# A bidirectional SSD layer: turnings of a tile in one step, TensorE's order tied at each chunk's scores, context products inside the main products

## The chip, the core and the metric

One core of a Trainium2 chip runs the kernel. The core has five engines with a queue of instructions each: TensorE (PE, matrix products and transposes by a product with the identity), VectorE (DVE), ScalarE (ACT), GpSimd (POOL) and SyncE (SP, which issues DMAs). Each engine takes its instructions in the order of its queue and waits on semaphores for the results of the others. The metric is the device time of one execution in microseconds. 0.5% of it is 9 us.

## The reference

Two layers over 1024 latent positions of width 1024 and a prefix of 256 context positions: layer 0 is gated windowed attention, layer 1 a gated bidirectional Mamba-2 mixer (SSD). Only layer 1 matters here. Per head group g of 8 (four heads of 64, state 128, chunks of 128):

```python
def ssd_mixer(h_lat, h_ctx, w_in, conv_w, conv_b, dt_bias, a_log, d_skip, norm_w, w_out, need_ctx_out):
    def front(h):
        z, xbc, dt_raw = jnp.split(h @ w_in, [SSD_WIDTH, SSD_WIDTH + SSD_CONV_DIM], axis=-1)
        xbc = jax.nn.silu(centred_depthwise_conv(xbc, conv_w, conv_b))   # 5 taps
        xs, bm, cm = jnp.split(xbc, ...)
        ...
    z_c, xs_c, b_c, c_c, dt_c = front(h_ctx)
    z, xs, bm, cm, dt = front(h_lat)
    y_c_f, s_f = scan_dir(xs_c, b_c, c_c, dt_c, 0, h0, need_ctx_out)
    y_c_b, s_b = scan_dir(xs_c, b_c, c_c, dt_c, 1, h0, need_ctx_out)
    y_f, _ = scan_dir(xs, bm, cm, dt, 0, s_f, True)
    y_b, _ = scan_dir(xs, bm, cm, dt, 1, s_b, True)
    # back: u = (y_f + y_b + d_skip * xs) * silu(z), RMS norm per group, @ w_out
```

A chunk's output is y_diag, the product of the scores cm @ bm^T (weighted by decays) with xs, and y_off, the product of cm with the state ahead of the chunk. The context gives the states with which the two scans begin.

## The kernel before

Every product in float32 is made of three products of split halves: weight high by input high, weight high by input low, weight low by input high (`wh`, `wl` and `uH`, `uL`).

For each group g, the generator `front(g)` makes what the scan needs. It has four tiles of 128 channels, in the order bT, x0, x1, cT, and then two gate tiles z. For a tile the *main product* is 48 matmuls of 128x512 over the 1024 latent positions (L1095), into a two-bank PSUM buffer `pj2`, of which there are two. For bT, x0 and x1 there is also a *context product*, 24 matmuls of 128x256 (L1085), into `psD`, one bank of PSUM and the only one of its name. A product is followed by the convolution (first tap on ScalarE, L1007; four taps on VectorE, L1011), by SiLU (tanh on ScalarE, L1018; product on VectorE, L1019) and, for bT, x0 and x1, by `natural`: turnings (transposes by TensorE, L1058) of the channel tile back into position-major form, into the same PSUM buffer, and copies by ScalarE (L1061) into `bn` or `xn`. Each z tile is 96 matmuls of 128x256 (L1129) into `pj2`: the first z tile takes the buffer that tile x1 leaves, the second that of cT. The last two tiles of weights, for z, come as `wr` and are split into `wh` (ScalarE, L1034) and `wl` (VectorE).

The steps behind a product go into a queue `post`, from which `front`'s progress releases them: one step for every 0.5 us of TensorE's products, and `natural`'s steps at least LATE = 3.0 us after the step before them, one a time.

The scan of group g runs in eight calls of `slot`, one for each chunk of 128: the scores (L1247, into a bank of `psX`, of which there are three), the two state reads (L1249, L1250), the state update (L1256, L1257), the multiplication with the decays `M` (L1251; `M` itself comes from `merge` on VectorE, L1230, and from four exponentials on ScalarE, L1236), four products with `xn` (L1281), the gate and the norm (L1292, L1293, L1295, L1300), two transposes of the result (L1312) with a copy each (`uT`, L1313), which is written out by DMA. Between these steps `fill(x)` draws work of `front(g + 1)`, so that TensorE has products to do; in the last group the work is the output projection `ssd_out` (L1527). The states at the chunks' borders (L1198, each into `psD`, then L1202 or L1210) are made by another generator, `states`, once tile x1 has been released.

The program is built by a scheduler: it takes the instructions in program order with their dependencies and buffers, orders each engine's queue by its own estimate of when each could start, and sets the semaphores. So an instruction's place in a queue is not its place in the code. `issue_after` is a tie for the scheduler: what is issued inside it stands behind the named instruction in that instruction's own queue, and no semaphore is added.

## Time and profile before

| | us |
|---|---|
| three runs | 1805.05, 1812.2, 1811.74 (median 1811.74) |
| profiled execution, its time | 1807.02 |
| its span, first to last instruction | 1805.3 |
| attention and the rest ahead of the SSD layer's front(0) | about 0 to 745 |
| front(0), before any scan | about 745 to 849 |
| eight groups' scans, first scores to first scores | 849.3, 954.8, 1060.5, 1166.3, 1272.1, 1377.9, 1483.7, 1589.0 |
| first matmul of the gate tiles, groups 1 to 3 | 924.58, 1030.35, 1136.13 (105.78 apart) |
| last group's scan with the output projection | 1589 to about 1743, then the tail |

Group g's scan and group g + 1's front share a stretch of about 105.8 us. In the profile's rows a line number is that of the kernel before; names like `pj` stand for `pj2`, without buffer numbers; `[1.30 <-ACT xn L1061]` is the time that the engine stood idle ahead of an instruction, and the instruction whose end released it. TensorE's matmuls overlap a little, so the distance between two starts, not the duration, is the time that one costs.

### The profile page before, as it was taken

The page shows a single profiled execution, that of the slowest core. Times are in us where ns is not written, and L with a number is a line of the kernel's source. Part 1 is how long each engine was busy: PE and PEld are TensorE (multiplying, and loading weights), DVE is VectorE, ACT ScalarE, POOL GpSimd, SP SyncE. Part 2 cuts the span into 40 slices and gives each one's busy share as a digit, 9 for nine tenths or more (in the row PEclk, how much of TensorE's full clock was granted, in tenths as well). Part 3 has the DMA queues.
Part 4 walks back from the last instruction along what each step waited for, and adds up shares of the span by engine and source line. Part 5 has one row for each costly group of instructions (what it writes and reads, how often), then busy time and mean ns, then how long its engine had stood idle before and what let it go on. Part 6 is the DMA issues. An engine that isn't in the chain of part 4 may idle for free.

```text
span 1805.3 us, 28983 instructions
## 1 busy us (share of the span) xinstructions
PE 1739.6 (96%) x10319; PEld 1494.7 (83%) x10319; DVE 1181.8 (65%) x2115; ACT 867.1 (48%) x1906; POOL 799.0 (44%) x1068
## 2 busy tenths in 40 slices
PE   6899999999999999999999999999999999999997
PEld 2697788888888887778888898988889898888887
DVE  4634436778877885684776858577684867766734
ACT  3612237777777774452443525344353534544522
POOL 2331127555575545103454544645454464554411
PEclk9999999999999999999999999999999999999999
DMA  9558856444455436222222323222332322656533
GB/s 334 226 144 268 283 177 149 106 100 111 111 153 130 120 102 221 73 53 73 71 77 82 92 62 98 79 71 79 81 93 62 100 73 76 174 169 170 175 101 121
DMA packets 212495, 227.61 MB, mean 126 GB/s; under 512 B 16384, under 2 KB 149632, under 8 KB 212352
## 3 DMA queue, kind: packets, MB, share of 16 engines
q1 hardware_dynamic: 178288, 207.12, 38.0%
q0 software_dynamic: 34064, 18.65, 5.8%
q8 instruction: 81, 1.33, 0.3%
q14 instruction: 62, 0.51, 0.1%
HBM read 190.88 MB, written 35.13 MB: 125 GB/s over the span
## 4 chain that ended last, share of the span: by engine, by line
PE 81%; DVE 9%; ACT 4%; DMA 3%; issue 2%; SPq 1%; POOL 1%; DVEq 0%; ACTq 0%; POOLq 0%
PE pj L1095 17%; PE pj L1129 10%; PE pj L1527 7%; PE pj L246 6%; PE pj L247 6%; PE pj L248 6%; PE psD L1085 4%; PE psX L1281 3%; PE pt L684 3%; PE psD L1198 2%; PE pv L691 2%; PE pv L690 1%; PE S L659 1%; PE S L658 1%; PE psX L1249 1%
## 5 line engine op out<-in xcount | busy, mean ns | idle before, releaser
L246 PE MATMUL pj<-uH,wh 128*128 128x512 f32 (+1 forms) x712 | 257.4, 363 | 9.0 <-ACT uH L470 6.3
L247 PE MATMUL pj<-uL,wh 128*128 128x512 f32 (+1 forms) x712 | 243.3, 342 | 0.5 <-POOL uL L707 0.4
L248 PE MATMUL pj<-uH,wl 128*128 128x512 f32 (+1 forms) x712 | 242.4, 341 | 1.4 <-POOL wl L231 1.4
L1095 PE MATMUL pj<-uH,wl 128*128 128x512 f32 x512 | 172.7, 405 | 0.0
L1095 PE MATMUL pj<-uH,wh 128*128 128x512 f32 x512 | 171.4, 405 | 1.2 <-ACT bn L1061 0.7
L1095 PE MATMUL pj<-uL,wh 128*128 128x512 f32 x512 | 169.2, 402 | 0.0
L246 PEld LDWEIGHTS pj<-uH,wh 128*128 128x128 f32 x712 | 135.6, 191 | 36.2 <-ACT uH L470 7.7
L1129 PE MATMUL pj<-wh,uH 128*128 128x256 f32 x512 | 150.3, 294 | 9.1 <-ACT xn L1061 9.1
L1173 POOL TENSOR_TENSOR xw<-xn,dtdec 128x256 f32<-128x256 f32 x144 | 92.9, 650 | 141.6 <-PE psD L1198 107.1
L1129 PE MATMUL pj<-wh,uL 128*128 128x256 f32 x512 | 152.7, 298 | 0.0
L248 PEld LDWEIGHTS pj<-uH,wl 128*128 128x128 f32 x712 | 135.0, 190 | 18.6 <-POOL wl L231 2.3
L247 PEld LDWEIGHTS pj<-uL,wh 128*128 128x128 f32 x712 | 135.8, 191 | 16.0 <-issue 3.0
L1129 PE MATMUL pj<-wl,uH 128*128 128x256 f32 x512 | 146.7, 287 | 0.0
L689 DVE TENSOR_TENSOR pl<-pt,ph 128x512 fp32r<-128x512 f32 x168 | 114.1, 688 | 47.2 <-ACT ph L688 46.2
L231 POOL TENSOR_TENSOR wl<-wr,wh 128x512 fp32r<-128x512 f32 x76 | 100.2, 1322 | 86.1 <-ACT wh L229 85.2
L663 DVE CUSTOM_DVE_ANT_0 sm<-S,mask,nsink 128x640 f32<-128x640 f32 (+2 forms) x160 | 119.2, 773 | 19.8 <-PE S L659 12.6
L665 ACT ACTIVATE sm<-sm,nm 128x640 f32<-128x640 f32 (+2 forms) x160 | 118.6, 742 | 16.6 <-DVE nm L663 15.9
L688 ACT CAST ph<-pt 128x512 fp32r<-128x512 f32 x168 | 97.5, 586 | 56.0 <-PE pt L684 52.7
L229 ACT CAST wh<-wr 128x512 fp32r<-128x512 f32 (+1 forms) x116 | 74.7, 648 | 87.7 <-PE pj L247 63.5
L1095 PEld LDWEIGHTS pj<-uH,wl 128*128 128x128 f32 x512 | 95.3, 188 | 19.2
L1095 PEld LDWEIGHTS pj<-uL,wh 128*128 128x128 f32 x512 | 95.4, 188 | 18.7
L1129 PEld LDWEIGHTS pj<-wh,uH 128*128 128x128 f32 x512 | 98.7, 193 | 13.5 <-ACT xn L1061 12.1
(339 smaller groups left out, 4810.8 us busy)
## 6 DMA issues: line engine op xcount, KB each, us to landing
wr<-w_x SPq DMA_DIRECT2D x32, 512.0 KB, 4.6
M<-acs SPq DMA_DIRECT2D x64, 256.0 KB, 4.9
bw<-acs SPq DMA_DIRECT2D x64, 256.0 KB, 5.5
wr<-w_sk SPq DMA_DIRECT2D x24, 512.0 KB, 3.8
wr<-wg SPq DMA_DIRECT2D x40, 256.0 KB, 4.5
qs<-q POOLq DMA_DIRECT2D x40, 256.0 KB, 3.9
wada<-w_ada SPq DMA_DIRECT2D x16, 512.0 KB, 7.2
wr<-wq SPq DMA_DIRECT2D x32, 256.0 KB, 3.0
```

Source lines behind the costliest of these rows:

```text
L231: (eng or nc.vector).tensor_tensor(l, raw, h, op=ALU.subtract)
L246: self.nc.tensor.matmul(ps, lh, rh, start=first and i == 0, stop=False)
L247: self.nc.tensor.matmul(ps, lh, rl, start=False, stop=False)
L248: self.last_mm = self.nc.tensor.matmul(ps, ll, rh, start=False, stop=last and i == n - 1)
L663: nc.vector.tensor_tensor_reduce(out=sm[:, :W], in0=Sv, in1=self.mask[:, m0 : m0 + W], scale=-SCALE, scalar=self.nsink[:, 4 * j + r : 4 * ...
L665: nc.scalar.activation(sm[:, :W], sm[:, :W], AF.Exp, bias=nm[:, r : r + 1], scale=-1.0, accum_out=sums[:, r : r + 1])
L688: nc.scalar.copy(ph, ptf)
L689: nc.vector.tensor_sub(pl, ptf, ph)
L1095: nc.tensor.matmul(raw[:, 512 * i : 512 * i + 512], l[:, k, :], r[i][:, k, :], start=k + y == 0, stop=k == KT - 1 and y == 2)
L1129: nc.tensor.matmul(pj[:, c], l, r[:, k, :], start=c % 2 + q + k + y == 0, stop=c % 2 == 1 and q == 1 and k == 3 and y == 2)
L1173: nc.gpsimd.tensor_tensor(xw, X(st, c).rearrange("p (r h) -> p r h", r=R), self.dtdec[:, c, hd(d, g)].unsqueeze(2).broadcast_to([P, R, HP] ...
L1527: nc.tensor.matmul(banks[x], l[:, z, sl], r, start=k == 2 * qs[0] and y == 0, stop=k == 2 * qs[-1] + 1 and y == 2)
```

## The change

Three parts. (1) `natural` makes all turnings of a tile in one step and the copies in the steps behind it, where it made four turnings, a copy, four turnings, a copy. (2) `self.pe` remembers the last product matmul and `self.opened` a chunk's scores: the scores stand behind the last product drawn before them on TensorE's queue, and what a fill draws stands behind the chunk's scores. (3) Except in the very first tile, the context product is drawn in the middle of the tile's main product, ahead of k = 4 of 8, where it was drawn before the main product. The instructions are the same in number and shape.

```diff
--- before.py
+++ after.py
@@ -1051,19 +1051,15 @@
             return lambda: weights(a["w_z"][g, q], 4, 256)
 
         def natural(raw, acc, dst, o, n):
-            steps = []
-
-            def tr(lo, hi):
-                for x in range(lo, hi):
+
+            def tr():
+                for x in range(n):
                     nc.tensor.transpose(raw[:, x * P : (x + 1) * P], acc[:, x * P : (x + 1) * P], self.ident)
 
             def ev(d, lo, hi):
                 nc.scalar.copy(d[:, :, o : o + P], raw[:, lo * P : hi * P].rearrange("p (c n) -> p c n", n=P))
 
-            for d, lo, hi in dst:
-                steps.append(lambda lo=lo, hi=hi: tr(lo, hi))
-                steps.append(lambda d=d, lo=lo, hi=hi: ev(d, lo, hi))
-            return [(LATE, steps)]
+            return [(LATE, [tr] + [lambda d=d, lo=lo, hi=hi: ev(d, lo, hi) for d, lo, hi in dst])]
 
         tiles = [(16 + g, "bT"), (2 * g, 0), (2 * g + 1, 1), (24 + g, "cT")]
         st["xn"] = [t(p, [P, 4, R * HP], F32, "xn4") for _ in range(2)] + [t(p, [P, NCC, R * HP], F32, "xn2")]
@@ -1078,21 +1074,26 @@
             cur, w = w, (weights(a["w_dt"], KT, P) if g + n == 0 else loads[n + 1]())
             nat = {"bT": ("bn", 0), 0: ("xn", 0), 1: ("xn", P)}.get(kind)
             wh, wl = cur["h"], cur["l"]
-            if nat:
-                raw = t(ps, [P, 512], F32, "psD")[:, :CTX]
+            def ctx():
+                cr = t(ps, [P, 512], F32, "psD")[:, :CTX]
                 for k in range(KT):
                     for y, (l, r) in enumerate(((wh, uH), (wh, uL), (wl, uH))):
-                        nc.tensor.matmul(raw, l[:, k, :], r[2][:, k, :], start=k + y == 0, stop=k == KT - 1 and y == 2)
+                        self.pe = nc.tensor.matmul(cr, l[:, k, :], r[2][:, k, :], start=k + y == 0, stop=k == KT - 1 and y == 2)
                         yield N256
                 acc = t(pf, [P, CTX], F32, "cctx")
-                post.extend(self.taps(x, raw, acc, 0, CTX, CTX) + self.silu(raw, acc) + natural(raw, acc, [(st[nat[0]][2], 0, 2)], nat[1], 2))
+                post.extend(self.taps(x, cr, acc, 0, CTX, CTX) + self.silu(cr, acc) + natural(cr, acc, [(st[nat[0]][2], 0, 2)], nat[1], 2))
+
+            if nat and g + n == 0:
+                yield from ctx()
             raw = t(ps, [P, LAT], F32, "pj2")
             acc = t(pf, [P, LAT], F32, "cacc") if nat and kind != "bT" else t(p, [P, LAT], F32, kind)
             for q in ((0,), (1,)) if g == 0 and n == 0 else ((0, 1),):
                 for k in range(KT):
+                    if k == KT // 2 and nat and g + n > 0:
+                        yield from ctx()
                     for y, (l, r) in enumerate(((wh, uH), (wh, uL), (wl, uH))):
                         for i in q:
-                            nc.tensor.matmul(raw[:, 512 * i : 512 * i + 512], l[:, k, :], r[i][:, k, :], start=k + y == 0, stop=k == KT - 1 and y == 2)
+                            self.pe = nc.tensor.matmul(raw[:, 512 * i : 512 * i + 512], l[:, k, :], r[i][:, k, :], start=k + y == 0, stop=k == KT - 1 and y == 2)
                             yield N512
                     if k == 3 and (q[0] == 0 or g + n == 0):
                         post.extend(w["steps"])
@@ -1126,7 +1127,7 @@
                         u, v = uH[i][:, 4 * q + k, c * P : (c + 1) * P], uL[i][:, 4 * q + k, c * P : (c + 1) * P]
                         for y, (l, r) in enumerate(((u, ww["h"]), (u, ww["l"]), (v, ww["h"]))):
 
-                            nc.tensor.matmul(pj[:, c], l, r[:, k, :], start=c % 2 + q + k + y == 0, stop=c % 2 == 1 and q == 1 and k == 3 and y == 2)
+                            self.pe = nc.tensor.matmul(pj[:, c], l, r[:, k, :], start=c % 2 + q + k + y == 0, stop=c % 2 == 1 and q == 1 and k == 3 and y == 2)
                             yield N256
                 if i == 1 and q == 0 and g + 1 < G:
                     st["next"] = weights(a["w_x"][16 + g + 1], KT, P)
@@ -1244,7 +1245,8 @@
             if n + 2 < G * NCH:
                 bw[n + 2] = load_rows(n + 2, 1, "bw")
             pcb = t(ps, [P, 512], F32, "psX")[:, :P]
-            nc.tensor.matmul(pcb, st["bT"][:, cs], st["cT"][:, cs], start=True, stop=True)
+            with self.tc.issue_after(self.pe.ins):
+                self.opened = nc.tensor.matmul(pcb, st["bT"][:, cs], st["cT"][:, cs], start=True, stop=True)
             po = t(ps, [P, 512], F32, "psX")
             nc.tensor.matmul(po[:, :256], st["cT"][:, cs], flat(st["hf"]), start=True, stop=True)
             nc.tensor.matmul(po[:, 256:], st["cT"][:, cs], flat(st["hb"][c]), start=True, stop=True)
@@ -1358,11 +1360,12 @@
                 def run(until):
                     nonlocal spent
                     while spent < until:
-                        cost = next(work, None)
-                        if cost is None:
-                            return
-                        spent += cost
-                        post.run(cost)
+                        with self.tc.issue_after(self.opened.ins):
+                            cost = next(work, None)
+                            if cost is None:
+                                return
+                            spent += cost
+                            post.run(cost)
 
                 def tick():
                     nonlocal chain
@@ -1524,7 +1527,7 @@
                     for x in range(4):
                         sl = slice(x * P, (x + 1) * P)
                         for y, (l, r) in enumerate(((w["h"], hi), (w["h"], lo), (w["l"], hi))):
-                            nc.tensor.matmul(banks[x], l[:, z, sl], r, start=k == 2 * qs[0] and y == 0, stop=k == 2 * qs[-1] + 1 and y == 2)
+                            self.pe = nc.tensor.matmul(banks[x], l[:, z, sl], r, start=k == 2 * qs[0] and y == 0, stop=k == 2 * qs[-1] + 1 and y == 2)
                             yield N512
                         if x == 1 and z == 0 and j < len(ws):
                             post.extend(ws[j]["steps"])
```

What the scheduler makes of it is seen in three places of the built programs. Lines move by a little: L1061 becomes L1060, L1095 L1096, L1085 L1081, L1129 L1130, L1058 L1057, L1198 L1199, L1312 L1314, L1247 L1249, L1236 L1237, L1313 L1315, L1295 L1297, L1202 L1203.

The first place is ScalarE's queue ahead of the gate product of the second of the seven groups after the first. Before, from the copies of tile x1's first four turnings to the copy of its last four:

```order
L1061 COPY xn_2452_10689<-pj_2526_11107 128x4x128
L1061 COPY xn_2454_10691<-psD_11038 128x2x128
L1236 ACTIVATE M_11231<-M_11231,vf_8731 128x128 x4
L1313 ACTIVATE uT_11348<-psX_11347,nw_8727 128x128
L1034 COPY wh_11410<-wr_11399 128x1024
L1007 ACTIVATE cT_11245<-pj_2548_11244,cb_8724,cw_8721 128x1024
L1295 ACTIVATE y_2562_11318,ss_11376<-y_2156_8751 128x257
L1061 COPY xn_2453_10690<-pj_2526_11107 128x4x128
```

And now:

```order
L1315 ACTIVATE uT_11348<-psX_11347,nw_8727 128x128
L1034 COPY wh_11410<-wr_11399 128x1024
L1237 ACTIVATE M_11231<-M_11231,vf_8731 128x128 x4
L1007 ACTIVATE cT_11245<-pj_2548_11244,cb_8724,cw_8721 128x1024
L1297 ACTIVATE y_2562_11318,ss_11376<-y_2156_8751 128x257
L1060 COPY xn_2452_10689<-pj_2512_11038 128x4x128
L1060 COPY xn_2453_10690<-pj_2512_11038 128x4x128
L1203 COPY hx_11367<-psD_11365 128x256
```

The copy of the first four turnings stood ahead of the four `M`; now both copies of the tile stand behind `uT`, `wh`, `M`, `cT` and `y`. This order, with small shifts (`M` behind `cT` in two of them), is that of three of the seven groups. In the four others (here the group behind it) the copies stand ahead of `y` and `wh`, and `cT` comes later still:

```order
L1237 ACTIVATE M_12315<-M_12315,vf_8731 128x128
L1315 ACTIVATE uT_12432<-psX_12431,nw_8727 128x128
L1237 ACTIVATE M_12315<-M_12315,vf_8731 128x128 x3
L1060 COPY xn_2644_11773<-pj_2704_12122 128x4x128
L1060 COPY xn_2645_11774<-pj_2704_12122 128x4x128
L1297 ACTIVATE y_2754_12402,ss_12460<-y_2156_8751 128x257
L1034 COPY wh_12494<-wr_12483 128x1024
```

The second place is TensorE's queue at the same point of the first of these two groups. Before, the last product matmuls of tile cT, then the next chunk's scores and state reads between the last four turnings and the first gate matmul:

```order
L1095 MATMUL pj_2548_11244<-uH_2034_8170,wl_11171 128x512
L1095 MATMUL pj_2548_11244<-uH_2132_8670,wl_11171 128x512
L1247 MATMUL psX_11464<-cT_10161,bT_9663 128x128
L1058 MATMUL pj_2526_11107<-ident_63,cacc_11108 128x128 x4
L1249 MATMUL psX_11466<-hf_11314,cT_10161 128x256
L1250 MATMUL psX_11466<-hb_2395_10350,cT_10161 128x256
L1198 MATMUL psD_11301<-xw_11284,bn_2457_10694 128x256
L1312 MATMUL psX_11347<-ident_63,y_2155_8749 128x128
L1129 MATMUL pj_2582_11401<-wh_11295,uH_2034_8170 128x256
```

Now, from the transpose that the `uT` above waits for:

```order
L1314 MATMUL psX_11347<-ident_63,y_2155_8749 128x128
L1096 MATMUL pj_2548_11244<-uL_2035_8171,wh_11129 128x512
L1096 MATMUL pj_2548_11244<-uL_2133_8671,wh_11129 128x512
L1096 MATMUL pj_2548_11244<-uH_2034_8170,wl_11131 128x512
L1096 MATMUL pj_2548_11244<-uH_2132_8670,wl_11131 128x512
L1057 MATMUL pj_2512_11038<-ident_63,cacc_11039 128x128 x8
L1199 MATMUL psD_11365<-xw_11326,bn_2457_10694 128x256
L1314 MATMUL psX_11347<-ident_63,y_2155_8749 128x128
L1130 MATMUL pj_2582_11401<-wh_11295,uH_2034_8170 128x256
```

The eight turnings are together behind tile cT's last matmul; the scores and the state reads are no longer ahead of the gate product. In the four groups of the other kind the turnings stand ahead of tile cT's last four matmuls:

```order
L1314 MATMUL psX_12431<-ident_63,y_2155_8749 128x128
L1057 MATMUL pj_2704_12122<-ident_63,cacc_12123 128x128 x8
L1096 MATMUL pj_2740_12328<-uL_2035_8171,wh_12213 128x512
L1096 MATMUL pj_2740_12328<-uL_2133_8671,wh_12213 128x512
L1199 MATMUL psD_12449<-xw_12410,bn_2649_11778 128x256
L1096 MATMUL pj_2740_12328<-uH_2034_8170,wl_12215 128x512
L1096 MATMUL pj_2740_12328<-uH_2132_8670,wl_12215 128x512
L1314 MATMUL psX_12431<-ident_63,y_2155_8749 128x128
L1130 MATMUL pj_2774_12485<-wh_12379,uH_2034_8170 128x256
```

The third place is the context product of tile x0, on TensorE. Before, it follows the last matmuls of that tile's main product (three of them in the first rows), and a chunk's scores stand among the main product's matmuls:

```order
L1247 MATMUL psX_10942<-cT_10161,bT_9663 128x128
L1095 MATMUL pj_2492_10911<-uL_2133_8671,wh_10798 128x512
L1095 MATMUL pj_2492_10911<-uH_2034_8170,wl_10800 128x512
L1095 MATMUL pj_2492_10911<-uH_2132_8670,wl_10800 128x512
L1058 MATMUL psD_10697<-ident_63,cctx_10745 128x128 x2
L1312 MATMUL psX_10841<-ident_63,y_2155_8749 128x128
L1249 MATMUL psX_10944<-hf_10815,cT_10161 128x256
L1250 MATMUL psX_10944<-hb_2421_10489,cT_10161 128x256
L1058 MATMUL pj_2467_10746<-ident_63,bT_10747 128x128 x4
L1256 MATMUL psX_10948<-xw_10891,bn_2265_9617 128x256
L1281 MATMUL psX_10973<-xn_2262_9614,M_10758 128x64 x4
L1085 MATMUL psD_10873<-uH_1654_6747,wh_10798 128x256
```

Now it begins behind the main product's 24th matmul, and the second half of the main product follows its last:

```order
L1096 MATMUL pj_2489_10873<-uH_2034_8170,wl_10765 128x512
L1249 MATMUL psX_10922<-cT_10161,bT_9623 128x128
L1251 MATMUL psX_10924<-hf_10812,cT_10161 128x256
L1252 MATMUL psX_10924<-hb_2421_10489,cT_10161 128x256
L1096 MATMUL pj_2489_10873<-uH_2132_8670,wl_10765 128x512
L1081 MATMUL psD_10936<-uH_1654_6747,wh_10763 128x256
L1081 MATMUL psD_10936<-uL_1655_6748,wh_10763 128x256
L1081 MATMUL psD_10936<-uH_1654_6747,wl_10765 128x256
```

The scores now have the products ahead of them that were drawn before them, and those drawn after them behind them.

## The prediction

> **What bounds the kernel now.** I read the page first, then TensorE's waits in the scan of layer 1, then its busy time there in slices of 50 us.

> ```profile
> span 1805.3 us, 28983 instructions
> PE 1739.6 (96%) x10319; PEld 1494.7 (83%) x10319; DVE 1181.8 (65%) x2115; ACT 867.1 (48%) x1906; POOL 799.0 (44%) x1068
> PE 81%; DVE 9%; ACT 4%; DMA 3%; issue 2%; SPq 1%; POOL 1%; DVEq 0%; ACTq 0%; POOLq 0%
> ```

> ```profile
> PE pj L1129 <- ACT xn L1061: 9.1, 7, 1.3
> PE pj L1058 <- ACT xn L1061: 0.6, 1, 0.6
> ...
> 850.00:900.00 50.00, 50.00 (x274) 43.09 (x273) 35.66 (x62) 19.58 (x45) 21.98 (x31) 1.00 0.28 69
> 900.00:950.00 50.00, 48.70 (x335) 45.10 (x334) 35.64 (x59) 23.13 (x56) 28.71 (x40) 1.00 0.29 79
> ```

> TensorE (PE) is busy for 96% of the span and carries 81% of the last chain. The waits are those between 820 and 1590 us, where the change lies: nothing but 7 waits of 1.3 us, one in each group of heads, for an eviction of `xn` by ScalarE (the other row, 0.6, lies at the edge, before group 0). The slices say the same: 50.00 of 50.00 busy, then 48.70, so 1.30 idle. No operation is added or taken away, so TensorE's own work stays as it is, and all that the change can do is to shorten these waits or to make new ones. The gain is bounded by them.

> The wait of one group, on the two engines that meet there (start, duration, line):

> ```profile
> 919.39 0.39 PE L1058 MATMUL psD<-ident,cctx 128*128 128x128 f32 x2
> ...
> 920.59 0.62 PE L1095 MATMUL pj<-uH,wl 128*128 128x512 f32 x2
> 921.05 0.38 PE L1247 MATMUL psX<-cT,bT 128*128 128x128 f32 x2
> 921.27 0.60 PE L1058 MATMUL pj<-ident,cacc 128*128 128x128 f32 x4
> 921.70 0.60 PE L1249 MATMUL psX<-hf,cT 128*128 128x256 f32 x2
> ...
> 922.57 0.59 PE L1198 MATMUL psD<-xw,bn 128*128 128x256 f32 x2
> 923.00 0.27 PE L1312 MATMUL psX<-ident,y 128*128 128x128 f32 x1
> 924.58 0.39 PE L1129 MATMUL pj<-wh,uH 128*128 128x256 f32 x1 [1.30 <-ACT xn L1061]
> ```

> ```profile
> 919.81 0.37 ACT L1061 COPY xn<-psD 128x256 f32<-128x256 f32 x1 [0.50 <-PE psD L1058]
> 920.08 1.28 ACT L1236 ACTIVATE M<-M,vf 128x128 f32<-128x128 f32 x4
> 921.26 0.35 ACT L1313 ACTIVATE uT<-psX,nw 128x128 f32<-128x128 f32 x1
> 921.52 1.03 ACT L1034 CAST wh<-wr 128x1024 fp32r<-128x1024 f32 x1
> 922.45 1.20 ACT L1007 ACTIVATE cT<-pj,cb,cw 128x1024 f32<-128x1024 f32 x1
> 923.55 0.41 ACT L1295 ACTIVATE y<-y 128x257 f32<-128x257 f32 x1
> ...
> 923.95 0.57 ACT L1061 COPY xn<-pj 128x512 f32<-128x512 f32 x1
> 924.42 0.38 ACT L1202 COPY hx<-psD 128x256 f32<-128x256 f32 x1
> ```

> The gate product of the first z tile (L1129) needs the PSUM buffer that still holds tile x1's second four turnings. These are done at 921.70, but ScalarE takes its instructions in the order of its queue: four `M`, `uT`, a weight half `wh`, the first tap of `cT` and `y` stand ahead of the copy, which starts at 923.95. Pitches read from start to start: the four `M` 1.18, `uT` 0.26, `wh` 0.93, `cT` 1.10, `y` 0.40, an `xn` copy 0.47, and from its end to z 0.16. On TensorE one L1095 takes 0.23, one turning 0.11 (four from 921.27 to 921.70), one L1198 pair 0.43. Without the wait z would start one turning after 923.00, at 923.11; it starts at 924.58. So a group loses 1.47, seven lose 10.3 us.

> **The change, part by part.** All eight turnings of a tile now stand together, and both copies behind them; the order of the built program, shown above, says where. I walk each group with these pitches, counted from T, the end of tile cT's last main matmul (921.05 before).

> In three of seven groups (the first kind) ScalarE's queue reads `uT`, `wh`, four `M`, `cT`, `y`, `xn`, `xn`. The transpose that `uT` waits for stands four L1096 ahead of T, so it ends at T - 0.92; a result reaches ScalarE 0.20 later (the psD turnings end at 919.61, the copy starts at 919.81), so `uT` starts at T - 0.72. Then 0.26 + 0.93 + 1.18 + 1.10 + 0.40 + 0.47 + 0.47 + 0.16 = 4.97, and z may start at T + 4.25. Behind T TensorE has only eight turnings, a state pair and a transpose: 0.87 + 0.43 + 0.11 = 1.41. The wait grows to about 2.9: twice the old one, because the scores and the context reads that covered two thirds of a microsecond are now behind z, and because both copies, not one, stand at the end of that queue. 3 x 2.9 = +8.7. Bounds: 3 x 1.47 = 4.4, if ScalarE gets as far ahead as now, and 3 x 3.5 = 10.5, if one of the `M` comes late.

> In four of seven (the second kind) the queue reads `M`, `uT`, three `M`, `xn`, `xn`, and `y`, `wh`, `cT` come behind. Counted from the transpose's start: `uT` at 0.31, then 0.26 + 0.88 + 0.47 + 0.47 + 0.16, z at 2.55; TensorE has 0.11 + 0.87 + four L1096 (0.92) + 0.43 + 0.11 = 2.44. A wait of 0.1 by these pitches and 0.65 if each step also shows its whole latency; I take 0.4, +1.6 for four, bounds 0.4 and 2.6.

> So this stall costs -10.3 + 8.7 + 1.6 = 0.0: what four groups win, three give back.

> The long waits have a second price. Granted clock (the number before the DMA share) around earlier waits of TensorE:

> ```profile
> 53.79 1.65 PE L246 MATMUL pj<-uH,wh 128*128 128x512 f32 x3 [2.77 <-ACT uH L470]
> ...
> 53.50:54.00 0.50, 0.21 (x1) 0.21 (x2) 0.23 (x1) 0.50 (x2) 0.50 (x1) 0.58 1.03 422
> ...
> 56.50:57.00 0.50, 0.50 (x2) 0.36 (x2) 0.50 (x2) 0.50 (x2) 0.00 (x0) 0.51 1.05 426
> 57.00:57.50 0.50, 0.50 (x4) 0.38 (x3) 0.50 (x2) 0.50 (x1) 0.00 (x0) 1.00 1.02 418
> ...
> 81.50 0.39 PE L246 MATMUL pj<-wh,uH 128*128 128x256 f32 x1 [2.35 <-DVE rope_b L526]
> ...
> 79.00:80.00 1.00, 0.15 (x2) 0.00 (x0) 1.00 (x2) 0.00 (x0) 0.00 (x0) 1.00 0.00 0
> ...
> 81.00:82.00 1.00, 0.51 (x4) 0.51 (x5) 1.00 (x3) 0.16 (x1) 0.48 (x1) 1.00 0.00 0
> ...
> 817.19 0.66 PE L1058 MATMUL pj<-ident,cacc 128*128 128x128 f32 x4 [2.31 <-DVE cacc L1019]
> ...
> 818.00:818.50 0.50, 0.35 (x1) 0.36 (x2) 0.12 (x1) 0.50 (x2) 0.50 (x2) 0.67 0.46 136
> ...
> 824.50:825.00 0.50, 0.50 (x4) 0.50 (x4) 0.50 (x1) 0.00 (x0) 0.00 (x0) 0.51 0.00 0
> ```

> [...]

> No DMA belongs to a moved step; the weight halves (`wh` on ScalarE, its remainder on VectorE) are posted at the same matmul of a main product as before, and where they stand on ScalarE is in the walk.

> The other costs are small, and the first two are walked through the built order in the same way. **Tile bT's copies:** both now stand just ahead of tile x1's first main matmul, with slack from +0.35 to -0.2 a group. One copy is 0.47; I take +0.5 in all, bounds 0 and 2. **The first group:** three steps of the state chain now meet in the one psD buffer, and one pays a DVE step and a state pair.

> ```profile
> L1210 DVE TENSOR_TENSOR hb<-hb,psD 128x256 f32<-128x256 f32 x55 | 23.0, 418 | 74.2 <-PE psD L1198 70.9 <-POOL xs L1272 3.3
> L1313 ACT ACTIVATE uT<-psX,nw 128x128 f32<-128x128 f32 x110 | 40.0, 363 | 97.1 <-PE psX L1312 97.1
> L1292 DVE TENSOR_TENSOR y<-y,psX 128x256 f32<-128x256 f32 x56 | 23.1, 413 | 15.4 <-POOL y L1274 13.3 <-PE psX L1281 2.1
> ```

> 0.42 + 0.43 = +0.9, bounds 0 and 1.5. **The last group**, where the output projection fills: the next scores stand right behind the two transposes whose evictions (363 ns each) free their bank; 8 chunks with some 0.12 showing, +1.0, bounds 0 and 2. **The head** (front of group 0, which waits for VectorE at 817 in either order): +0.3, bounds -1 and 1.3. **The tie of the scores** and **the context product in the middle** cost nothing of themselves: DVE, ACT and POOL are busy 36, 23 and 29 of the 50 us in the slice above, and the psX evictions wait for TensorE (L1313 97.1, L1292 partly), not it for them. If this cover fails, see the third rival.

> Sum: 0.0 + 3.4 + 0.5 + 0.9 + 1.0 + 0.3 = +6.1 us. The profiled execution took 1807.02 (span 1805.3), so 1813.1 in its terms. The runs before were 1805.05, 1812.2 and 1811.74; with the profiled one their mean is 1809.0, below the median of 1811.74. I put the sum on that mean: 1815. All lower bounds together (-10.3 + 4.4 + 0.4 - 1 = -6.5) give 1802.5, all upper ones (-10.3 + 10.5 + 2.6 + 10.2 + 2 + 1.5 + 2 + 1.3 = +19.8) 1829.

> **The rivals.** 0.5% is 9 us, about what a measurement of this kernel can tell from no change.

> *Faster, by the vanished stall.* If in all seven groups the two copies are through before TensorE is ready, as the second kind nearly shows, 10.3 us go and no clock is lost: 1799. For it: the turnings are asked for earlier than now. Against it: in three groups `wh`, `M`, `cT` and `y` stand ahead of the copies, and an engine's queue is not overtaken. Even so it barely passes 9 us. 0.09.

> *Slower, by the clock.* Every long wait falls into one cell of the grid and the next cell stays slow too, as at 818: 10.2 instead of 3.4, sum +12.9, 1822. It decides once the idle time is above about 2.5, where the rows above put the limit; with the scores delayed further, the same wait would be 3.5 and the fall certain. For it: 2.77 was enough. Against it: at 53.58 one cell was enough, since TensorE was busy behind it, as it is in the z product. 0.22.

> *Slower, by the tie.* The scores of a chunk can't start before the last product matmul, nor the next fill before the scores. Where the bank that they need is still read (L1292, 413 ns), TensorE stands with nothing else to do, while now it has products to go on with. In half of 56 chunks 28 x 0.413 = 11.6, on top of 6.1: 1827. For it: the tie takes the freedom from the order to run products past scores whose bank isn't free. Against it: the 15.4 us of idle time before L1292 show VectorE ahead, not behind. It decides when an eviction comes later than half a microsecond after its matmul. 0.16.

> *No effect:* the scheduler had already moved the context products behind their main products, so the third part could be undone by it. The built order says that it isn't; but if nothing in it mattered, 1809. That lies within my forecast.

> **How the numbers follow.** Forecast 0.53 (no change beyond 9 us, the sum at +6), clock 0.22, tie 0.16, vanished stall 0.09. Faster by over 0.5%: 0.09; within: 0.53; slower: 0.22 + 0.16 = 0.38. The likeliest one's own range is 1803 to 1818; the range of 1803 to 1828 takes in both slower rivals and leaves out the fast one and the far end of the tie.

> **What would show it.** Seven waits of L1130 for L1060: four below 0.7 and three between 2.5 and 3.2, by turns and beginning with a short one; a granted clock of 0.5 behind some of the three; z tiles that begin 104.7 and 107.2 us after the one of the group before by turns (104.3 of work and the wait), a lost clock on top. No waits of the scores L1249 above 0.3. I am wrong on the mechanism if the seven waits are alike, on the clock if it is 1.00 all through 850 to 1590, and on the tie if the scores or the fill's matmuls show waits of several us in sum.

## The result and the profile after

The changed kernel takes 1816.96 us (median of 20 runs, 1809.9 to 1820.61) against 1807.87 (20 runs, 1804.85 to 1812.2): a ratio of 1.0041, 95% interval 1.0031 to 1.0052, so slower, by 0.4%. The two medians lie 9.1 us apart, which is 0.50%, the two means 7.8. The profiled execution took 1810.52, its span is 1808.1. It is one of the fastest of the 20, which turns out to matter.

From the page, and from TensorE's waits between 820 and 1600 us (total, times, longest):

```profile
span 1808.1 us, 29027 instructions
PE 1738.9 (96%) x10319; PEld 1496.9 (83%) x10319; DVE 1183.0 (65%) x2115; ACT 871.5 (48%) x1906; POOL 794.0 (44%) x1068
...
PE pj L1130 <- ACT xn L1060: 10.6, 5, 2.9
PE pj L1530 <- ACT wh L1462: 0.9, 1, 0.9
PE psD L1199 <- DVE hb L1211: 0.6, 1, 0.6
```

TensorE's busy time is that of before (1739.6), and the counts of instructions that do work are the same; the 44 more of the page are semaphore instructions. The seven alike waits have become five of three kinds, the first one in the head. Those of the scan, from TensorE's timeline:

```profile
925.33 0.39 PE L1130 MATMUL pj<-wh,uH 128*128 128x256 f32 x1 [0.59 <-ACT xn L1060]
1032.42 0.39 PE L1130 MATMUL pj<-wh,uH 128*128 128x256 f32 x1 [2.89 <-ACT xn L1060]
1243.76 0.39 PE L1130 MATMUL pj<-wh,uH 128*128 128x256 f32 x1 [2.88 <-ACT xn L1060]
1455.10 0.39 PE L1130 MATMUL pj<-wh,uH 128*128 128x256 f32 x1 [2.89 <-ACT xn L1060]
```

ScalarE ahead of the second of them:

```profile
1027.69 1.06 ACT L1034 CAST wh<-wr 128x1024 fp32r<-128x1024 f32 x1
1028.65 1.27 ACT L1237 ACTIVATE M<-M,vf 128x128 f32<-128x128 f32 x4
1029.83 1.19 ACT L1007 ACTIVATE cT<-pj,cb,cw 128x1024 f32<-128x1024 f32 x1
1030.92 0.41 ACT L1297 ACTIVATE y<-y 128x257 f32<-128x257 f32 x1
1031.22 0.19 ACT L1297 ACTIVATION_READ_ACCUMULATOR y<-y 128x1 f32 x1
1031.32 1.05 ACT L1060 COPY xn<-pj 128x512 f32<-128x512 f32 x2
```

It works without a pause through the queue that the built order showed, and both copies stand at its end. Three groups wait 2.9 us, one 0.59, three not at all, and behind the long ones the clock stayed at 1.00 in this execution. The gate products of group 1 begin at 925.33, of group 7 at 1559.26, by turns 104.16 and 107.18 us apart (105.78 each before): from group 1 to group 7 633.93 us against 634.67. The scans themselves neither win nor lose. From 825.93 to 1798.73 the clock is 1.00.

The head does lose. TensorE at the wait for tile x1's SiLU in group 0, and the granted clock behind it (the number before the DMA share):

```profile
816.74 1.97 PE L1057 MATMUL pj<-ident,cacc 128*128 128x128 f32 x8 [4.84 <-DVE cacc L1019]
...
816.00:817.00 1.00, 0.26 (x1) 0.27 (x2) 0.85 (x2) 1.00 (x9) 0.00 (x0) 0.50 0.43 103
...
824.00:826.00 2.00, 2.00 (x12) 2.00 (x11) 0.75 (x1) 0.00 (x0) 0.00 (x0) 0.52 0.00 0
```

The wait is 4.84 where it was 2.31, and the clock is at half speed from 815.7 to 825.9, 10.2 us instead of 6.8. The head's own length is read from where the front of group 0 begins (a wait for `cacc` of L923, first row of each pair) to the first scores; the changed kernel, then the kernel before:

```profile
736.82 0.50 PE L246 MATMUL pj<-uH,wdth 128*128 128x512 f32 x1 [1.40 <-ACT cacc L923]
848.98 0.38 PE L1249 MATMUL psX<-cT,bT 128*128 128x128 f32 x2
...
740.00 0.50 PE L246 MATMUL pj<-uH,wdth 128*128 128x512 f32 x1 [1.46 <-ACT cacc L923]
849.29 0.38 PE L1247 MATMUL psX<-cT,bT 128*128 128x128 f32 x2
```

112.16 against 109.29, +2.9. TensorE comes to its wait at the same point (75.1 and 74.9 us after the front's beginning), but what it waits for is 2.7 us later: VectorE's L1019 stands behind the merge of L1231, which waits for GpSimd's addition to `bw` (L1227, before L1226), which waits for the load of `bw`, a DMA:

```profile
813.26 1.04 POOL L1227 TENSOR_TENSOR bw<-bw,vd 128x512 f32<-128x512 f32 x1 [75.10 <-DMA bw<-acs]
...
813.97 1.04 POOL L1226 TENSOR_TENSOR bw<-bw,vd 128x512 f32<-128x512 f32 x1 [72.63 <-DMA bw<-acs]
```

That is 76.4 us after the front's beginning in the changed kernel and 74.0 in the kernel before, 2.5 later. 1.6 of it comes from the clock at the front's beginning. Just behind the wait for L923 the changed kernel's clock is 0.5 from 737.18 to 740.60 and TensorE makes 6 products in 2 us, while the kernel before keeps its clock and makes 9:

```profile
737.00:739.00 2.00, 2.00 (x6) 1.57 (x7) 0.97 (x1) 0.99 (x2) 1.02 (x1) 0.55 0.59 147
...
740.00:742.00 2.00, 2.00 (x9) 1.64 (x10) 0.79 (x1) 1.18 (x2) 1.02 (x1) 1.00 0.51 168
```

So the writes of `acs`, which need these products, begin 55.7 us after the front's beginning instead of 54.1. The wait ahead of it is about as long as before (1.40 and 1.46) but lies otherwise on the grid of 3.41 us: TensorE is idle for 1.40 us of the cell that ends at 737.18, in the kernel before for 1.11 of the one that ends at 739.66. So this isn't the work of the change: ten of the fourteen profiles have this stretch and put the writes at 55.5 to 55.7, among them kernels that load `bw` as before; the four others (the kernel before, the turnings alone, and two of the kernels below with the change's group 0) have none and put them at 54.1. The other 0.9 comes behind the writes. SyncE's queue, of the changed kernel and then of the kernel before:

```profile
792.48 4.14 SPq L941 DMA_DIRECT2D acs<-sz  x8
...
800.39 2.34 SPq L952 DMA_DIRECT2D eald<-tot  x1
...
804.65 0.51 SPq L1222 DMA_DIRECT2D bw<-acs  x1
```

```profile
794.12 4.14 SPq L941 DMA_DIRECT2D acs<-sz  x8
...
802.01 0.42 SPq L952 DMA_DIRECT2D eald<-tot  x1
...
804.37 1.09 SPq L1221 DMA_DIRECT2D bw<-acs  x1
```

The load of `bw` is issued 12.2 us after the writes of `acs` instead of 10.3, because one small write of `eald` holds the queue for 2.34 us instead of 0.42; it has landed 20.6 us after them instead of 19.7. The order of that queue is the same in both. This execution came to the front 3.2 us earlier, in layer 0, which the change doesn't touch, and that hides the loss in its span. From group 7's gate products to the last matmul of the output projection it is 187.07 (1559.26 to 1746.33) against 184.77 (1559.25 to 1744.02), +2.3, of which 0.92 is the wait for `wh` of L1462 and 0.5 a wait of the scores for `uT`; the remaining 0.9 isn't traced. From the first scores to group 1's gate products it is 76.35 against 75.29, +1.1. Behind the last matmul the tail is 0.5 longer.

### The profile page after: what moved, and what is told of

The parts are those of the page before. It is cut to its first block, busy times and chain, and to the rows that moved or that the text cites. A ratio compares the mean times of both kernels' runs of the same rounds, so it can differ in the third digit from the quotient of the medians.

```text
span 1808.1 us, 29027 instructions
## 1 busy us (share of the span) xinstructions
PE 1738.9 (96%) x10319; PEld 1496.9 (83%) x10319; DVE 1183.0 (65%) x2115; ACT 871.5 (48%) x1906; POOL 794.0 (44%) x1068
## 3 DMA queue, kind: packets, MB, share of 16 engines
q8 instruction: 81, 1.33, 0.3%
## 4 chain that ended last, share of the span: by engine, by line
PE 80%; DVE 9%; DMA 4%; ACT 3%; issue 2%; SPq 1%; POOL 0%; DVEq 0%; ACTq 0%; POOLq 0%
PE pj L1096 17%; PE pj L1130 10%; PE pj L1530 7%; PE pj L246 6%; PE pj L247 6%; PE pj L248 6%; PE psD L1081 4%; PE psX L1283 3%; PE pt L684 3%; PE psD L1199 2%; PE pv L691 2%; PE psX L1252 2%; PE psX L1251 2%; PE pv L690 1%; PE S L659 1%
## 5 line engine op out<-in xcount | busy, mean ns | idle before, releaser
L246 PE MATMUL pj<-uH,wh 128*128 128x512 f32 (+1 forms) x712 | 257.3, 363 | 6.3 <-ACT uH L470 3.7
L1096 PE MATMUL pj<-uH,wh 128*128 128x512 f32 x512 | 172.4, 409 | 1.2 <-ACT bn L1060 1.2
L1096 PE MATMUL pj<-uH,wl 128*128 128x512 f32 x512 | 171.8, 404 | 0.0
L1096 PE MATMUL pj<-uL,wh 128*128 128x512 f32 x512 | 169.3, 404 | 0.0
L246 PEld LDWEIGHTS pj<-uH,wh 128*128 128x128 f32 x712 | 135.6, 191 | 33.9 <-issue 6.3
L1130 PE MATMUL pj<-wh,uH 128*128 128x256 f32 x512 | 151.1, 295 | 10.6 <-ACT xn L1060 10.6
L1130 PE MATMUL pj<-wl,uH 128*128 128x256 f32 x512 | 152.3, 297 | 0.0
L1130 PE MATMUL pj<-wh,uL 128*128 128x256 f32 x512 | 151.6, 296 | 0.0
L247 PEld LDWEIGHTS pj<-uL,wh 128*128 128x128 f32 x712 | 135.7, 191 | 16.0 <-DVE uL L471 3.2
L1315 ACT ACTIVATE uT<-psX,nw 128x128 f32<-128x128 f32 x128 | 46.7, 365 | 179.5 <-PE psX L1314 179.3
L663 DVE CUSTOM_DVE_ANT_0 sm<-S,mask,nsink 128x640 f32<-128x640 f32 (+2 forms) x160 | 119.1, 772 | 19.8 <-PE S L659 12.7
L1096 PEld LDWEIGHTS pj<-uH,wl 128*128 128x128 f32 x512 | 95.9, 188 | 19.6
L1130 PEld LDWEIGHTS pj<-wh,uH 128*128 128x128 f32 x512 | 99.0, 193 | 14.5 <-ACT xn L1060 13.3
```

The lines of the kernel that those rows point to most:

```text
L246: self.nc.tensor.matmul(ps, lh, rh, start=first and i == 0, stop=False)
L247: self.nc.tensor.matmul(ps, lh, rl, start=False, stop=False)
L663: nc.vector.tensor_tensor_reduce(out=sm[:, :W], in0=Sv, in1=self.mask[:, m0 : m0 + W], scale=-SCALE, scalar=self.nsink[:, 4 * j + r : 4 * ...
L1096: self.pe = nc.tensor.matmul(raw[:, 512 * i : 512 * i + 512], l[:, k, :], r[i][:, k, :], start=k + y == 0, stop=k == KT - 1 and y == 2)
L1130: self.pe = nc.tensor.matmul(pj[:, c], l, r[:, k, :], start=c % 2 + q + k + y == 0, stop=c % 2 == 1 and q == 1 and k == 3 and y == 2)
```

## The experiments

"Before" of each group of runs is the kernel before on the same chip. Each ratio has its 95% interval behind it.

**The parts alone and in pairs.** The diff of the change, taken apart: the first part is `natural`, the second the ties, the third `ctx()` ahead of k = 4.

> The kernel before with the first part alone (all turnings of a tile in one step). In the built order the eight turnings of x1 then stand ahead of context or main products in six or seven groups, so z finds its buffer free. My theory (time is the sum of the waits for that copy, plus clock lost behind waits above about 2.5 us): waits of the z line for the xn copy near 0 in most groups, no granted clock below 1.00 between 850 and 1590, 5 to 10 us faster than before (1798 to 1803). Rival (the long run-to-run spread comes from the head or the output projection, not from these waits): the time stays within 3 us of before.

> The changed kernel without its third part (context products ahead of the main products in program order again, turnings together and ties kept). Built order: turnings, a transpose, a state pair and two main matmuls ahead of z, the four M and both copies at the end of ScalarE's queue, alike in the groups. My theory: seven alike waits of 0.3 to 1.2 us, none above 2.5, so no clock lost in the scan: between 8 us faster and 2 us slower than before. Rival (the ties, not the waits at z, cost the time): as slow as the changed kernel, +6 to +10.

> The changed kernel without its second part (no ties of scores and fills). Built order: turnings well ahead of z, behind them main or context products. My theory: waits at z near 0, no clock lost in the scan, 5 to 10 us faster than before. Rival (ties are free, and what costs is the context product in the middle): no faster than before.

> The changed kernel without its first part (turnings in two steps of four again, ties and middle kept). Built order: the first tap of cT, four M, the norm's scaling and the first copy stand ahead of the last copy in all seven groups. By the same walk z waits 2.9 us in six or seven groups: +8 to +10 us against before from the waits themselves. My theory adds clock lost behind about half of them, 1.7 to 3.4 us each: +14 to +23 in all, with the granted clock 0.004 to 0.008 lower than that of before and runs that differ by several us. Rival (such waits cost only their own length): +8 to +10 and the same clock as before.

> The kernel before with the second part alone (ties of scores and fills). Built order: turnings in two steps of four, a state pair between or behind them, and ScalarE's queue with the first tap of cT, uT and the norm's scaling ahead of the last copy. By the walk z waits about 1.8 us in five groups. My theory: +2 to +4 from that, and as in the changed kernel without joint turnings (waits of 2.1 for the copies of bn and 3.1 at the turnings, 47 us in all) two waits a group at the turnings and at the next main product, where the tie leaves TensorE nothing else: +10 to +45. Rival (the ties are free by themselves): within 4 us of before.

> The kernel before with the third part alone (context products in the middle of the main products in program order). Built order around z as before, in all seven groups: one wait of 1.3 us each. My theory: within 4 us of before, no clock lost in the scan. Rival (the product in the middle delays the main product's end and with it the turnings): waits at the turnings as without the joint turnings, +10 or more.

| parts in | median, us | before, us | ratio |
|---|---|---|---|
| turnings | 1828.18 | 1811.29 | 1.0096 (1.0077 to 1.0114) |
| ties | 1858.83 | 1810.42 | 1.0265 (1.0244 to 1.0286) |
| middle | 1810.03 | 1810.57 | 0.9998 (0.9983 to 1.0013) |
| turnings, ties | 1843.81 | 1811.29 | 1.0172 (1.0155 to 1.019) |
| turnings, middle | 1846.1 | 1811.29 | 1.0189 (1.0172 to 1.0207) |
| ties, middle | 1858.85 | 1811.29 | 1.0268 (1.0251 to 1.0285) |
| all three | 1816.96 | 1807.87 | 1.0041 (1.0031 to 1.0052) |

The first four expectations were wrong, three of them in sign and the fourth, right in sign, in size and place. They reckoned only with z, where the waits did become small (0.9, 4.9, 1.3 and 0.8 us in all, in the order of the texts above). The fifth, for the ties alone, came out a little above its range (+48), the sixth, for the middle alone, as expected. TensorE's waits between 820 and 1640 us, first with the turnings alone, then with turnings and ties, then with ties and middle (the single waits for `xw`, 5.4 and 6.0, lie in the head):

```profile
PE psD L1194 <- DVE hb L1206: 5.9, 4, 2.6
PE psD L1194 <- POOL xw L1169: 5.4, 1, 5.4
PE psD L1194 <- ACT hx L1198: 5.1, 2, 3.4
```

```profile
PE psD L1081 <- ACT xn L1060: 15.3, 7, 2.5
PE psD L1057 <- DVE cctx L1019: 6.5, 1, 6.5
PE psD L1194 <- POOL xw L1169: 6.0, 1, 6.0
PE pj L1125 <- ACT xn L1060: 4.9, 8, 0.7
```

```profile
PE pj L1058 <- ACT xn L1061: 21.3, 8, 3.1
PE pj L1100 <- ACT bn L1061: 12.7, 6, 2.1
```

With the turnings alone nothing keeps the fills behind the scores: the gate products of groups 1 to 5 are 102.4 to 105.1 us apart, less than before, while the scan falls behind. Group 6's first scores come 16.1 us after its last gate matmul starts, group 7's 17.1 us (0.12 in the kernel before), and from group 7's gate products to the end of the projection it takes 206.3 us instead of 184.8, with the state chain (L1194) run without cover. Turnings and middle without the ties are alike: 210.1 us for that last part. With turnings and ties but without the middle, a context product in each of six groups waits 2.48 us for psD to be copied out (L1081), a wait of which the changed kernel shows nothing in the scan. With ties and middle but turnings in two steps, turnings wait 2.2 to 3.1 us for a copy of `xn` in each group, and main products 2.1 us for one of `bn`; 13 stretches of half speed of 3.4 us follow (mean clock of the profile 0.978, against 0.993 in that of the kernel before), some 20 of the 47 us. So with any one part left out the other two make waits that it removes, and no part's worth can be told from it alone.

**The change again,** for another position of its waits on the clock's grid.

> The changed kernel once more, for another position of its waits on the clock's grid. My theory: the same waits of 0.6, 0, 2.9, 0, 2.9, 0, 2.9 at the z line, and clock lost in the scan where more than about 1.9 of a wait's 2.9 us falls into one grid cell of 3.41 us (1.84 did not, 1.97 did in the runs so far), so about 2 of 3: one or more stretches of half speed of 3.4 us between 1020 and 1600 in the profile, single runs between 1808 (clock 0.991 or more) and 1820 (0.987), the time falling with the recorded clock by 1.7 to 2 us for each 0.001. Rival (the run-to-run spread is not clock): the clock is the same in fast and slow single runs.

1822.19 against 1810.42, ratio 1.0057 (1.0037 to 1.0078). The three long waits and the clock behind them, second profile:

```profile
1040.38 0.39 PE L1130 MATMUL pj<-wh,uH 128*128 128x256 f32 x1 [2.89 <-ACT xn L1060]
...
1042.00:1044.00 2.00, 2.00 (x11) 2.00 (x10) 1.96 (x2) 0.00 (x0) 0.00 (x0) 0.50 0.20 64
1044.00:1046.00 2.00, 2.00 (x13) 1.82 (x13) 0.91 (x2) 1.03 (x1) 0.62 (x1) 0.78 0.00 0
...
1253.27 0.58 PE L1130 MATMUL pj<-wh,uH 128*128 128x256 f32 x1 [2.88 <-ACT xn L1060]
...
1254.00:1256.00 2.00, 2.00 (x12) 2.00 (x11) 1.97 (x2) 0.16 (x1) 0.19 (x1) 0.50 0.76 261
...
1466.03 0.39 PE L1130 MATMUL pj<-wh,uH 128*128 128x256 f32 x1 [2.88 <-ACT xn L1060]
...
1466.00:1468.00 2.00, 1.98 (x16) 1.98 (x17) 1.93 (x3) 0.92 (x3) 0.62 (x1) 1.00 0.88 306
```

Two of three waits are followed by 3.4 us at half speed, and the next group's gate products come 105.71 and 105.58 us later, not 104.17: about 1.5 us each. In the first profile none of the three was followed by it:

```profile
1032.00:1034.00 2.00, 1.58 (x13) 1.58 (x14) 1.93 (x3) 1.30 (x4) 0.67 (x2) 1.00 0.78 279
1034.00:1036.00 2.00, 2.00 (x17) 1.95 (x17) 1.96 (x2) 0.00 (x0) 0.54 (x1) 1.00 0.21 65
```

The same wait, the same kernel, another place on the grid: counted from each profile's own onsets of half speed, the most of a wait that lies in one cell is 1.69, 1.48 and 1.78 us in the first profile, and 2.31, 2.69 and 1.58 in the second. Over the 27 single runs of the two measurements the time rises by 1.9 us with each 0.001 of mean clock lost (a straight line through them, correlation 0.86): 1809.9 to 1811.37 at 0.991, 1817.86 to 1822.22 at 0.987. So most of the spread of the runs goes with the clock; 1811.58 at 0.993 and 1822.34 at 0.988 stand 3 and 4 us off that line.

**A shorter wait, and none.** Ties on ScalarE behind the last `xn` copy (`self.lastc`), on top of the change:

```diff
-            post.extend(self.taps(x, raw, acc, 0, LAT, LAT) + self.silu(raw, acc))
+            steps = self.taps(x, raw, acc, 0, LAT, LAT) + self.silu(raw, acc)
+            if kind == "cT" and g:
+                def first(f=steps[0]):
+                    with self.tc.issue_after(self.lastc.ins):
+                        f()
+                steps[0] = first
+            post.extend(steps)
```

> The changed kernel with one tie more: on ScalarE the first tap of cT stands behind the last copy of tile x1 (groups 1 to 7). By the walk the three long waits lose one tap (1.1 us) and become 1.7 to 1.8, just below what has cost clock so far. My theory: 3.4 us less from the waits, and nearly no clock lost in the scan, another 3 to 4: 1809 to 1811, about the time of before. Rival (only the length of the waits counts): 3.4 us less than the changed kernel, with its clock.

1810.98 against 1810.42, ratio 1.0005 (0.999 to 1.002), 11 us below the change in the same runs.

```profile
PE pj L1136 <- ACT xn L1060: 7.3, 5, 1.8
PE pj L1057 <- DVE cacc L1019: 5.8, 1, 5.8
```

The three waits are 1.79 each (the 5.8 is the head's); two kept the clock, one lost it. The two profiles (spans 1821.8 and 1814.3) differ by 7.5: 4.6 in the seven groups, which is 3.3 for three waits shorter by 1.1 and one stretch of lost clock, and 1.9 behind them. The medians differ by 11; what is beyond 7.5 isn't settled.

With the same tie on the split of all z weights as well:

> The changed kernel with two ties more: the first tap of cT and the split of the z weights stand behind the last copy of tile x1 on ScalarE. Built order: in all seven groups the turnings stand seven main matmuls ahead of z, and the copies behind the four M. By the walk the copies end 2.85 us after the transpose ahead of the turnings began and TensorE is ready at 3.1: no wait. My theory: seven waits of 0 to 0.2, no clock lost in the scan, 10.3 - 2.7 = 7 to 8 us faster than before (1799 to 1803). Rival (the wait moves on: weights split later make z itself or the second z tile wait for wh or wl): a new wait of 1 us or more in each group, the time of before or slower.

1819.33, ratio 1.0053 (1.0034 to 1.0071): the rival. The wait for the copy is gone from the scan, and two of 0.9 us in each group have come for the weights, which are now split too late.

```profile
PE pj L1140 <- ACT wh L1036: 6.4, 7, 0.9
PE pj L1140 <- DVE wl L1042: 6.1, 7, 0.9
```

With the tie on the second z tile's weights alone, and with the exponentials and the norm tied instead:

> The changed kernel with the first tap of cT and the split of the second z tile's weights only behind the last copy of tile x1. Built order: six of seven groups have the turnings behind cT's last matmul, and M and y ahead of the copies. By the walk (0.26 + 1.18 + 0.40 + 2 x 0.47 + 0.16 from T - 0.72, at T + 2.4 to 2.6 against 1.41) a wait of 1.0 to 1.2 us in six groups, no new wait for weights. My theory: 6 x 1.1 + 2.7 - 10.3 = -1 us against before, no clock lost in the scan: within 3 us of before. Rival (waits for wh and wl again, 1.8 a group): +9 as with both weights tied.

> The changed kernel with three ties on ScalarE: the first tap of cT, each chunk's exponentials of M and the norm's squares stand behind the newest copy of turned halves. Built order: in groups 2 to 7 the turnings of x1 stand some 3.3 us of TensorE's work ahead of z and both copies directly behind uT, with the z weights split long before. By the walk (0.2 + 2 x 0.47 + 0.16 = 1.3 us) no wait at z in six groups, up to 1 us in the first. My theory: no clock lost in the scan, 6 to 9 us faster than before. Rival (a new wait takes its place, as when the z weights were split late): the M exponentials come later and the chunk's products L1287 or the scores wait for them, 0.5 us or more a chunk: slower than before.

The first gave 1812.22 against 1810.57, 1.0004 (0.9988 to 1.0021), with 105.12 us between gate products (105.78 before) and no lost clock between 833 and 1800. The waits at z are 0.9 (0.6 in group 1), and from group 1 to group 7 4.0 us are won (630.7 against 634.7); the head (111.61 against 109.29) and the last group (186.87 against 184.77) give them back. The second gave 1816.77, 1.0027 (1.0009 to 1.0046); no wait at z from group 2 on, but a new one of 1.65 in six groups, at another tile's main product and not where the rival had it:

```profile
PE pj L1096 <- ACT xn L1060: 9.9, 6, 1.6
```

**Head and scan mended together.** The kernel with the tie on cT and on the second z tile's weights, and turnings in two steps in group 0 only:

```diff
+            if g == 0:
+                steps = []
+                for d, lo, hi in dst:
+                    steps.append(lambda lo=lo, hi=hi: tr(lo, hi))
+                    steps.append(lambda d=d, lo=lo, hi=hi: ev(d, lo, hi))
+                return [(LATE, steps)]
```

> The kernel with both ties on ScalarE (first tap of cT and split of the second z tile's weights behind the last copy) and, in group 0 alone, the turnings in two steps of four as before. My theory: the head is as long as in the kernel before (first scores 109.3 to 110.6 us after the wait for cacc L923 at the front's beginning, against 111.6 to 112.5 with joint turnings), with half speed for 6.8 us and not 10.2 there; z tiles 105.1 apart instead of 105.8; so 2 us less than with the two ties alone, and 2 to 5 us faster than before (ratio 0.997 to 0.999). Rival (the head's length comes from the ties or the tile order, not from the joint turnings): first scores at 111.6 or later, and the time of before.

1808.35 (1803.39 to 1809.94) against 1809.7, ratio 0.9987 (0.9974 to 1.0): at the edge of what can be told, and the only kernel here whose interval doesn't reach above 1. That is 2.4 us by the ratio and 1.4 by the medians, where 2 to 5 were expected. The head is 110.59 us (742.42 to 853.01), with the stretch of half speed at the front's beginning, as in the middle alone (110.58); half speed behind the wait for `cacc` lasts 6.8 us again, and the scan's waits are small:

```profile
PE pj L1146 <- ACT xn L1064: 5.8, 7, 0.9
PE pj L1061 <- DVE cacc L1019: 2.6, 1, 2.6
```

## Why the prediction was right, and where not

**Right, the waits at z.** Three of about 2.9 and four small ones were forecast; they were 2.89, 2.88, 2.89 and 0.59, 0, 0, 0, by turns and beginning with a short one. The z tiles were to come 104.7 and 107.2 us apart and came 104.16 and 107.18. The stall's sum was to be 0.0; the waits sum to 9.25 against 9.1, and group 1 to group 7 differ by -0.7. That ScalarE's queue decides is also shown by the runs in which ties were added on that queue alone (1.79, 0.9, and none for the copy with all z weights tied).

**Right, and mis-sized in one step: the clock.** The grid was right and the price nearly (1.5 against 1.7). The step that failed is the limit of about 2.5 us in one cell. The prediction's own rows only put it between 1.74, which did nothing, and 2.56 (51.02 to 53.58), and it took the upper end; the runs put it between 1.65 and 1.85 (counted in the last section). In the pair of ties and middle, 2.11 and in one case 1.77 in one cell was followed by half speed, 1.85 was not; with the shorter wait 1.79 was and 1.73 was not. With a limit of 1.75, the middle of these, and cells of 3.41 a wait of 2.9 loses the clock in some four fifths of its positions, an estimate, rather than in a third to three quarters. "Two of three" came out as none in the first profile, where the clock is 1.00 all through 850 to 1590, the prediction's sign of being wrong, and as two in the second. The second rival, a loss every time and twice as long, didn't come in either: behind z TensorE is busy, and in the second profile one stretch of 3.4 us ended it each of the two times.

**Wrong in size: the head.** It was forecast at +0.3, at most +1.3, and was +2.9 (112.53 in the second profile, +3.2). The step that failed is that group 0 "waits for VectorE at 817 in either order". It does, but not at the same time: VectorE itself hangs on the load of `bw`. From the merge to the first scores it is 34.65 and 34.11 us in the two profiles of the change, 34.24 before, 33.83 and 33.73 in the middle alone and the last mended kernel, with turnings in two steps there, so what stands behind the merge costs some 0.5, near the forecast, the third stretch of half speed included. The rest lies ahead of the merge, and in the two profiles that were compared 1.6 of it is the clock at the front's beginning and not the change. With the same clock there, the change's group 0 still costs 1.6 to 2.3: 111.53 and 111.61 in the two later kernels without that stretch against 109.29 before, 112.16 to 112.53 with it against 110.58 and 110.59. That is seen in SyncE's queue: `bw` was issued 12.0 to 12.5 us after the writes of `acs` in six of the seven profiles with joint turnings and the middle in group 0 (10.9 in the one with copies first), and 10.25 to 10.8 in the seven others. Why one small write waits longer there, with the same order of that queue, is open. Behind the longer wait the clock is at half speed for a third stretch: TensorE is idle for 3.41, 1.04 and 1.33 us of the cells from 812.28, 815.69 and 819.11, in the kernel before for 2.61 and 0.61 of those from 814.75 and 818.17 and for nothing of the next.

**Wrong in place: the last group.** +1.0 was forecast for the evictions of `uT`; +2.3 came, 0.46 of it from `uT` (a wait of the scores above the 0.3 that the prediction allowed) and 0.92 (2.2 in the second profile) from the first weights of the projection, which the prediction left out. **The first group** was to cost 0.9 beside the wait at z. It came 1.1 longer although that wait is 0.7 shorter, so 1.8; 0.6 of it is the wait for `hb` shown above, and the stretch also holds 14 records of state products against 6, so part of it is work moved from elsewhere. **Tile bT's copies** were to cost 0.5 and cost nothing: no main product of the scan waits for them.

Together, without clock lost in the scan: +2.9 + 1.1 - 0.7 + 2.3 + 0.5 for the tail = 6.1, where the prediction had 2.7; with 3.4 for the clock it had 6.1, and the means differ by 7.8, the medians by 9.1. So the sum was too low by a fifth to a third, within its range. The forecast of no change beyond 0.5% held by the ratio, whose interval ends at 0.52%; the medians lie just on the border (0.50%). So it held narrowly and with some luck: the head and the last group together were 3.9 us above their terms, and the weights of the projection and the tail had no term at all.

**The rivals.** The stall did not vanish in all groups. The ties did not make the scores wait (0.5 us in all) in the changed kernel; alone they cost 48 us, but at the turnings, at z and in the state chain, not at the scores' bank. That the change might do nothing is excluded by the result's interval, and that its third part might do nothing by turnings and ties without it (1.0172) and with it (1.0041).

## What to carry to other kernels

When a scheduler orders the queues, walk the built queue of the engine that releases the bottleneck, with start-to-start pitches of the old trace: here that gave a wait of 2.9 us to within 0.1 before anything ran. Look at head and tail with the same care as at the loop, since a wait there that grew by 2.5 us cost more than the loop as a whole; and before such a difference is put down to the change, compare the clock ahead of it. Don't value the parts of a reordering one by one: here one alone costs 17 us, another 48, the third nothing, and all three together 9.

## What was not expected of the hardware

In the first profile of the change half speed comes, up to 1795 us, in stretches of 3.41, 6.83 and 10.24 us, and the onsets lie on one grid: counted from the first, they come 8, 209 and 232 times 3.413 us later. In the second they come 9, 17, 210, 233, 297, 359 and 463 times 3.413 us later. What follows is a count over the fourteen profiles of this case, from 60 to 1795 us and leaving out the front's beginning. A cell is a stretch of 3.413 us of the grid, its idle time the time in it without a product or turning on TensorE. Every one of the 60 cells at full speed with 1.9 us or more of idle time was followed by half speed (the one from 814.75 in the kernel before, with 2.61, is one of them), 10 of the 27 with 1.65 to 1.85 were (the one from 1450.57 in the first profile of the change, with 1.78, was not), and none with less, among them 95 with 1.0 or more. The front's beginning doesn't go with these counts: there 1.20 to 1.44 was followed by half speed in ten profiles (1.40 in the first of the change) and 1.11 was not in the kernel before. Ahead of that wait stand eight products of a single column (128x1, 0.95 us), which the profile counts as busy; whether they count as idle for the clock is not shown.

A cell already at half speed was followed by another with less idle time than that: in the kernel before, the cell from 818.17 holds one wait of 0.61 and the clock stays at half speed through the next. Of the cells at half speed, all 31 with 0.6 or more of idle time were followed by another, and none of the 88 with 0.50 or less.

In the pair of turnings and ties the groups are 109.24 us apart, 32 cells, so the waits of all groups lie at one place of the grid, and all six waits of 2.48 us were followed by half speed.
